# Rotating images by 90 degrees: all loads ahead of the stores, on one DMA queue, through twelve reused buffers

## The chip, the cores and the metric

The kernel runs on one core of one Trainium2 chip. The metric is the device time of one execution in microseconds (us); the time before is the median of 5 runs. A profile of one execution comes beside it. Engines in the profile: DVE is VectorE, ACT is ScalarE, SP is SyncE, POOL is GpSimd. Here only DVE computes; SP and ACT do nothing but issue DMAs, and the DMA engines, 16 of them, carry the data between HBM and SBUF.

## What is computed

A batch of 32 images with 3 channels of 256 x 256 float32 is rotated clockwise, each of the 96 planes by itself:

```python
batch, c, h, w = 32, 3, 256, 256
x = np.random.randn(batch, c, h, w).astype(np.float32)
out = np.rot90(x, k=-1, axes=(-2, -1)).astype(np.float32)
```

So out[i, j] = x[255 - j, i] in each plane: no arithmetic, 25.17 MB in and 25.17 MB out.

## The kernel before

The 96 planes are cut into 12 slabs of 8 planes, 2 MB each; the loop `for n in range(n_slabs)` takes one after the other. A slab passes through three steps.

Load (L47): two DMAs of 1 MB from SP's queue. Each fills every second partition of the input tile, 64 of them, with 16 consecutive rows of a plane, which is one run of 16 KB (`RI` = 16 rows of 256 floats).

Turn (L53): 8 transposes on VectorE, one for each c of `RO` = 8. A transpose works on blocks of 32 x 32 inside a group of 32 partitions; 512 elements of each partition go into one. The access patterns of source and destination do the rest: the destination is written backwards, which makes a rotation out of the transposition. The output tile holds, for each half `i` of the slab, 8 consecutive output rows in each of 128 partitions.

Store (L56): two DMAs of 1 MB from ACT's queue, each with 128 runs of 8 KB.

Tiles come from two pools, `in_pool` and `out_pool`, of 6 buffers each (16 KB in a partition, 192 KB together). The first 6 slabs can be loaded without waiting for a buffer; slab 6 goes into the buffer of slab 0, and so has to wait until slab 0 has been turned. The turn of slab 6 likewise waits until slab 0 has been stored. The order on each queue is the program's: SP holds 24 loads, ACT 24 stores, and each queue's instructions are issued in order, one standing until what it waits for has come. The framework that sets the waits hands out 8 completion semaphores for DMAs in turn; a DMA that gets a semaphore that is still in use waits for the DMA that used it before. With both queues drawing from the 8, SP has 6 loads on their way before it waits for the first.

Of the kernel before, what the change touches and what calls it, by code (L numbers as in the profile page):

```python
# [1 line left out]

# [4 lines left out]


@with_exitstack  # L10
def kernel(
    ctx: ExitStack,
    tc: tile.TileContext,
    x: bass.AP,
    out: bass.AP,
):

    nc = tc.nc
    fp32 = mybir.dt.float32

    B, C, H, W = x.shape
    P = nc.NUM_PARTITIONS
    RI, RO = 16, 8  # L30
    K, G = H // RI, H // RO
    I = 2
    Q = P // (K * I)
    n_slabs = B * C // (Q * I)

    ld_v = x.rearrange("b c h w -> (b c h) w").rearrange(
        "(n i m r) w -> n i m (r w)", i=I, m=Q * K, r=RI)
    st_v = out.rearrange("b c h w -> (b c h) w").rearrange(
        "(n i p c) w -> n i p (c w)", i=I, p=P, c=RO)

    in_pool = ctx.enter_context(tc.tile_pool(name="in_pool", bufs=6))
    out_pool = ctx.enter_context(tc.tile_pool(name="out_pool", bufs=6))

    for n in range(n_slabs):
        t_in = in_pool.tile([P, RI * W], fp32, tag="t_in")
        for i in range(I):
            nc.sync.dma_start(out=t_in[i::I], in_=ld_v[n, i])  # L47

        t_out = out_pool.tile([P, I, RO * W], fp32, tag="t_out")
        src = t_in.rearrange("p (r g c) -> p c r g", r=RI, c=RO)  # L50
        dst = t_out.rearrange("p i (c k r) -> p c r k i", c=RO, r=RI)[:, :, ::-1, ::-1, :]
        for c in range(RO):
            nc.vector.transpose(out=dst[:, c], in_=src[:, c])  # L53

        for i in range(I):
            nc.scalar.dma_start(out=st_v[n, i], in_=t_out[:, i])  # L56


# [1 line left out]
_INS = ['x']  # L60
_OUTS = [((32, 3, 256, 256), 'float32')]


# [23 lines left out]
```

## Time and profile before

| | |
|---|---|
| median of 5 runs | 124.46 us (124.43 to 124.56) |
| the profiled execution | 124.43 us |
| its span in the profile | 122.6 us |
| VectorE busy | 96.3 us in 96 transposes, 1091 ns mean |
| DMA | 50.34 MB, mean 410 GB/s over the span |
| loads: issue to landing, median | 15.0 us |
| stores: issue to landing, median | 12.5 us |
| SP's issue of a load | 472 ns median, 617 longest |
| ACT's issue of a store | 338 ns median, 1225 longest |
| first load issued | 0.73 us |
| first transpose starts | 8.45 us |
| first store issued | 16.65 us |

The span runs from the first to the last instruction of the profiled execution. Consecutive transposes overlap, so that 96 of them take 96.3 us and not 96 times their mean. In the profile's row of 40 slices a slice is 3.066 us; a digit is the busy share in tenths, 9 standing for 90% and more. In a list of waits the columns are: who waited for what, total us, how many times, the longest.

### The profile page before, as it was taken

To read this page: it belongs to the slowest core of one execution; us is meant where nothing else is said; L and a number is where in the kernel's file an instruction comes from. 1 tells how busy PE (TensorE), PEld (TensorE's weight loads), DVE (VectorE), ACT (ScalarE), POOL (GpSimd) and SP (SyncE) were. 2 spreads that over 40 slices of the span, in tenths; PEclk is the share of its full clock that TensorE was granted. 3 is DMA by queue.
4 is the path that set the end of the run, shared out by engine and by line. 5 is a ranking of instruction groups with operands and counts; after the bars stand their busy time and mean duration, and the time that the engine had idled before them with its cause. 6 is when DMAs were issued, how large, how long until landed. Compare 5 with 4: busy or idle time off the path is not lost.

```text
span 122.6 us, 225 instructions
## 1 busy us (share of the span) xinstructions
DVE 96.3 (79%) x96; POOL 0.2 (0%) x4
## 2 busy tenths in 40 slices
DVE  0029999999999999999999999999999999100000
POOL 0000000000000000000000000000000000000000
DMA  3999999999999999999999999999999999999993
GB/s 85 422 428 428 428 433 339 428 433 409 428 449 428 409 444 430 425 436 411 449 428 428 425 430 444 428 412 425 428 428 428 428 428 428 428 428 428 428 428 160
DMA packets 5377, 50.34 MB, mean 410 GB/s; under 512 B 768, under 2 KB 768, under 8 KB 768
## 3 DMA queue, kind: packets, MB, share of 16 engines
q1 hardware_dynamic: 1920, 25.17, 48.9%
q10 hardware_dynamic: 3456, 25.17, 48.6%
q14 instruction: 1, 0.01, 0.0%
HBM read 25.17 MB, written 25.17 MB: 410 GB/s over the span
## 4 chain that ended last, share of the span: by engine, by line
DMA 58%; DVE 24%; DVEq 1%; issue 1%; SPq 0%; ACTq 0%
DMA out_dram<-t_out 53%; DVE t_out L53 24%; DMA t_in<-in_x_dram 6%; DVEq L82 1%; SPq L47 0%; ACTq L56 0%; DVEq L53 0%
## 5 line engine op out<-in xcount | busy, mean ns | idle before, releaser
L53 DVE STREAM_TRANSPOSE t_out<-t_in 128x512 f32<-128x512 f32 x96 | 96.3, 1091 | 8.5 <-DMA t_in<-in_x_dram 8.5
L71 POOL MEMSET const-bfloat16-1.0<- 128x1 bf16 x1 | 0.1, 102 | 0.0
L71 POOL MEMSET const-uint8-127<- 128x1 uint8 x1 | 0.1, 102 | 0.0
L71 POOL MEMSET const-float32-0.0<- 128x1 f32 x1 | 0.1, 99 | 0.2 <-issue 0.2
L71 POOL MEMSET const-float32-1.0<- 128x1 f32 x1 | 0.1, 99 | 0.0
## 6 DMA issues: line engine op xcount, KB each, us to landing
t_in<-in_x_dram SPq DMA_DIRECT2D x24, 1024.0 KB, 15.0
out_dram<-t_out ACTq DMA_DIRECT2D x24, 1024.0 KB, 12.5
```

The source lines that it names most:

```text
L53: nc.vector.transpose(out=dst[:, c], in_=src[:, c])
L71: nc = _bacc.Bacc("TRN2", target_bir_lowering=False, num_devices=1)
L82: with _tile.TileContext(nc) as tc:
```

## The change

The two pools become 12 single buffers of 16 KB in a partition, `units`, the same 192 KB. Slab n is loaded into unit n, for n = 0 to 10, before anything else is issued; no load waits for a buffer. Slab n is turned out of unit n into unit n - 1, which the turn of slab n - 1 has just read; slab 0 is turned into unit 11. Each slab is stored from the unit into which it was turned. Slab 11 is loaded into unit 11, after slab 0 has been stored from it; this load is issued behind the stores of slabs 0 and 1.

All DMAs are now issued by SP: 22 loads, 5 stores (slab 0 has three, since its first half is cut into a piece of 1 KB and one of 7 KB in each partition), 2 loads, 20 stores. ACT's queue is empty. With 8 semaphores for one queue, each DMA from the ninth on waits for the one 8 places before it, apart from what it waits for otherwise.

Slab 0 has a layout of its own: each half is loaded into one half of the unit, with 8 rows (a run of 8 KB) in each of 128 partitions, and is turned by two transposes of 1024 elements a partition, of which the first waits only for its half. So slab 0 has 4 transposes instead of 8; the other slabs have 8 as before. On VectorE the first transpose of each later slab also waits for the last of the slab before.

```diff
-    ld_v = x.rearrange("b c h w -> (b c h) w").rearrange(
-        "(n i m r) w -> n i m (r w)", i=I, m=Q * K, r=RI)
-    st_v = out.rearrange("b c h w -> (b c h) w").rearrange(
-        "(n i p c) w -> n i p (c w)", i=I, p=P, c=RO)
+    N_UNITS = 12
+    rows_in = x.rearrange("b c h w -> (b c h) w")
+    rows_out = out.rearrange("b c h w -> (b c h) w")
+    ld8_v = rows_in.rearrange("(n i p r) w -> n i p (r w)", i=I, p=P, r=RO)
+    ld16_v = rows_in.rearrange("(n i m r) w -> n i m (r w)", i=I, m=Q * K, r=RI)
+    st_v = rows_out.rearrange("(n i p c) w -> n i p (c w)", i=I, p=P, c=RO)
 
-    in_pool = ctx.enter_context(tc.tile_pool(name="in_pool", bufs=6))
-    out_pool = ctx.enter_context(tc.tile_pool(name="out_pool", bufs=6))
+    pools = [ctx.enter_context(tc.tile_pool(name=f"unit{u}", bufs=1)) for u in range(N_UNITS)]
+    units = [p.tile([P, RI * W], fp32, name=f"u{u}") for u, p in enumerate(pools)]
 
-    for n in range(n_slabs):
-        t_in = in_pool.tile([P, RI * W], fp32, tag="t_in")
+    def load(n, t):
         for i in range(I):
-            nc.sync.dma_start(out=t_in[i::I], in_=ld_v[n, i])
+            if n == 0:
+                nc.sync.dma_start(out=t.rearrange("p (i f) -> p i f", i=I)[:, i], in_=ld8_v[n, i])
+            else:
+                nc.sync.dma_start(out=t[i::I], in_=ld16_v[n, i])
 
-        t_out = out_pool.tile([P, I, RO * W], fp32, tag="t_out")
+    def turn(n, t_in, t_out):
+        if n == 0:
+            for i in range(I):
+                fs = slice(i * RO * W, (i + 1) * RO * W)
+                src = t_in[:, fs].rearrange("p (r g c) -> p c r g", r=RO, c=RO)
+                dst = t_out[:, fs].rearrange("p (c g r) -> p c r g", c=RO, r=RO)
+                dst = dst[:, :, ::-1, ::-1]
+                for h in range(2):
+                    cs = slice(h * RO // 2, (h + 1) * RO // 2)
+                    nc.vector.transpose(out=dst[:, cs], in_=src[:, cs])
+            return
         src = t_in.rearrange("p (r g c) -> p c r g", r=RI, c=RO)
-        dst = t_out.rearrange("p i (c k r) -> p c r k i", c=RO, r=RI)[:, :, ::-1, ::-1, :]
+        dst = t_out.rearrange("p (i c k r) -> p c r k i", i=I, c=RO, r=RI)[:, :, ::-1, ::-1, :]
         for c in range(RO):
             nc.vector.transpose(out=dst[:, c], in_=src[:, c])
 
+    def store(n, t):
         for i in range(I):
-            nc.scalar.dma_start(out=st_v[n, i], in_=t_out[:, i])
+            src = t.rearrange("p (i f) -> p i f", i=I)[:, i]
+            cuts = [0, W, RO * W] if n == i == 0 else [0, RO * W]
+            for a, b in zip(cuts, cuts[1:]):
+                nc.sync.dma_start(out=st_v[n, i][:, a:b], in_=src[:, a:b])
+
+    last = N_UNITS - 1
+    for n in range(n_slabs - 1):
+        load(n, units[n])
+    for n in range(n_slabs):
+        turn(n, units[n], units[(n - 1) % N_UNITS])
+        store(n, units[(n - 1) % N_UNITS])
+        if n == 1:
+            load(n_slabs - 1, units[last])
```

## The prediction

> **What bounds the kernel now.** I read the page first: busy time by engine, then the slices, then the queues.
>
> ```profile
> DVE 96.3 (79%) x96; POOL 0.2 (0%) x4
> ...
> DVE  0029999999999999999999999999999999100000
> ...
> DMA  3999999999999999999999999999999999999993
> GB/s 85 422 428 428 428 433 339 428 433 409 428 449 428 409 444 430 425 436 411 449 428 428 425 430 444 428 412 425 428 428 428 428 428 428 428 428 428 428 428 160
> ...
> q1 hardware_dynamic: 1920, 25.17, 48.9%
> q10 hardware_dynamic: 3456, 25.17, 48.6%
> ```
>
> The DMA row is 9 in every slice but the first and the last: the 16 DMA engines are what the kernel runs at. VectorE (DVE) is idle for the first 8 us and the last 18. Loads (q1) and stores (q10) move 25.17 MB each, and together their packets fill 97.5% of the engines' span. What a change can win is therefore not inside the 38 full slices, except where the rate falls: slice 6 (from 18.4 us) has 339 where its neighbours have 428 to 433. The rates on either side of 428 further on (409 beside 449) cancel.
>
> The chain of waits should not mislead here:
>
> ```profile
> DMA out_dram<-t_out 53%; DVE t_out L53 24%; DMA t_in<-in_x_dram 6%; DVEq L82 1%; SPq L47 0%; ACTq L56 0%; DVEq L53 0%
> ```
>
> It gives VectorE 24%, but the slices show DMA full beside those transposes; nothing becomes shorter by shortening them.
>
> Next I cut the span at the places where the traffic changes its kind, and asked for the busy time of each stretch (columns: stretch, length, DVE, POOL, clock, DMA share, GB/s).
>
> ```profile
> 0.00:2.00 2.00, 0.00 (x0) 0.20 (x4) 1.00 0.00 0
> 2.00:3.20 1.20, 0.00 (x0) 0.00 (x0) 1.00 0.87 218
> 3.20:18.20 15.00, 9.75 (x10) 0.00 (x0) 1.00 1.02 433
> 18.20:24.20 6.00, 6.00 (x7) 0.00 (x0) 1.00 0.96 370
> 24.20:54.20 30.00, 30.00 (x31) 0.00 (x0) 1.00 1.01 431
> 54.20:84.20 30.00, 30.00 (x31) 0.00 (x0) 1.00 1.01 428
> 84.20:120.20 36.00, 20.58 (x21) 0.00 (x0) 1.00 1.01 427
> 120.20:122.60 2.40, 0.00 (x0) 0.00 (x0) 1.00 0.23 96
> ```
>
> From 3.2 to 18.2 us only loads run, from 24.2 to 84.2 loads and stores mixed on two queues, from 84.2 on almost only stores. The three rates, 433, 431 and 428, 427, differ by no more than packets at the edges of a stretch explain, so I take one rate for all, 429 GB/s. With it the span is accounted for: 2.0 us before the first byte; 0.59 lost in the 1.2 us at 218; 50.33 MB / 429 = 117.3; the dip around 18 to 24 us; and at the end 2.4 us that move only 0.23 MB (0.54 us' worth), so 1.86. The dip I price on the slices, whose edges fall better: slices 1 to 7 average 415.1 against 428.5, over 7 x 3.066 us that is 0.67. Sum 2.0 + 0.59 + 117.3 + 0.67 + 1.86 = 122.4, and 0.2 that I cannot place, to the span of 122.6. That profiled execution took 124.43 us, so 1.83 lie around the span; the median of the runs is 124.46, no different.
>
> Last, who waits:
>
> ```profile
> SPq L47 <- DMA t_in<-in_x_dram: 57.7, 18, 6.3
> SPq L82 <- DMA out_dram<-t_out: 50.4, 4, 43.2
> ```
> ```profile
> DVE t_out L53 <- DMA t_in<-in_x_dram: 8.5, 1, 8.5
> ```
>
> SyncE's queue (SP) waits 57.7 us for earlier loads while DMA is full: it is simply ahead. These waits are free, and VectorE waits only for the first slab.
>
> **The change part by part.**
>
> *The traffic.* Bytes are the same. Loads: 22 of 24 keep their 16 KB runs; slab 0's two load with 8 KB runs. Stores: 24 become 25, 128 small (1 KB) runs are added. q10's 3456 packets of 8 KB and completions took 48.6% of the span, q1's 1920 of 16 KB and completions 48.9%, for the same bytes: run length from 8 KB up changes nothing by more than 0.3 points (0.4 us over all the data), and a twelfth of the loads is concerned, so 0.03 us. The 128 extra runs are 8 per DMA engine, 1 completion more each: at the mean length of a q10 packet (0.486 x 16 x 122.6 us / 3456 = 276 ns) that would be at most 9 x 0.28 = 2.5 us if short ones cost as much as long ones; since both queues' time goes with bytes, not packets (1920 against 3456), I take 0.03 and keep 0.5 as upper end.
>
> *The order on one queue.* The stores leave ACT's queue for SP's. The dip falls where the first stores (issued at 16.65 us) join the running loads on a second queue. In the changed kernel no two queues run together, so I take its 0.67 away; the bounds are 0.67 and nothing (if it is the first store as such that costs it, it moves to 56 us).
>
> In its place come three turns of direction in one queue: loads to stores, stores to the last load, load to stores. The trace has no such turn on one queue. The nearest row is 84.2, where mixed traffic becomes pure stores: 428 before, 427 after, and the slices there (425, 428) show no dip, so one turn costs under 0.05 us. The far one is the dip, 0.67 each, 2.0 for three. The first is nearer in kind for two of the turns; for the turn back to loads neither is. I take 0.2 for all three, with 0 and 2.0 as ends.
>
> *Where the stream could run dry.* Data start at an effective 2.6 us (2.0 + 0.59). 22 loads (23.07 MB) end at 56.4, store 0 (2.1 MB, 4.9 us) at 61.3, store 1 at 66.2, the last load at 71.1, and store n from 2 on starts at 71.1 + 4.9 x (n - 2): store 11 at 115.2, its end at 120.1.
>
> The last load is a new wait: it fills unit 11, which store 0 reads, so SP stands until store 0 has landed, and behind it in SP's order are stores 2 to 11. What covers it is store 1, issued ahead and worth 4.9 us. Needed: landing, at most about 0.9 us after the last byte (two loads, 4.9 us of data from 2.6, end at 7.5; VectorE starts at 8.45), 0.5 for SP's issue (median 472 ns), and 1.3 from the first issue (0.73) to the first bytes (2.0): 2.7. Price nothing, reserve 2.2. Without cover it would cost those 2.7. [...]
>
> Beyond that SP carries 49 issues: 24 loads at 0.47 us, 25 stores at ACT's 338 ns (median) to 1225 (longest): 20 to 42 us in all, of 120. Each DMA from the ninth on waits for the one eight before it; eight megabyte transfers are 19.6 us of queued work, more than the 15.0 median to landing with which the queue is full today. Price nothing.
>
> *VectorE.* It starts earlier, since slab 0's halves are turned one by one: first half in at 2.6 + 2.45 + 0.9 = 6.0. Its four transposes of 1024 elements are not in the trace; by elements they are twice 1.003 us (96.3 / 96), together 8.0. Slab 0 ends near 14. The other 11 take 8.03 each, and each now waits for the one before to finish, 0.15 more (a transpose lasts 1091 ns and the next starts after 1003): the last ends near 104, against 115.2 when its store's turn comes. 11 us of reserve cover every sensible price of the new shape: even at twice the time it is 8 more. Nothing.
>
> *Loads alone.* The stretch with loads alone grows from 15 us to 54. The row says 433 for 15 us, and I keep 429. [...]
>
> *Start and end.* The first load has 128 runs instead of 64, so its engines may fill sooner or later: -0.1, bounds -0.3 and +0.1. The tail's 1.86 includes engines that finish one after another; without the dip they should stay closer: -0.1, bounds -0.4 and +0.3.
>
> **Sum.** 122.6 - 0.67 + 0.03 + 0.03 + 0.2 - 0.1 - 0.1 = 122.0; plus 1.83: 123.8 us. Its own range, without the far ends, is 123.2 to 124.2.
>
> **The rivals.**
>
> *Nothing changes.* The dip belongs to the first stores, not to the second queue, and comes at 56 us instead. For it: it lies exactly at the first stores. Against it: the stores were issued two microseconds earlier, and the loads were what moved in it. 122.0 + 0.67 = 122.7, 124.5 us. Chance 0.18.
>
> *Each turn costs a dip.* Place: 56.4, 66.2 and 71.1 us, where the queue changes direction. Price 0.67 each, 2.0 in all instead of the 0.2: 123.8, so 125.6 us. It decides from 0.35 each on: 1.05 in all takes up the 0.8 that the other terms win and 0.25 more. For it: the only dip of the trace is at a change of kind. Against it: the change at 84 us shows none. Chance 0.13.
>
> *A stall at the last load, or slower loads.* If store 0 lands over 2.2 us later than assumed, each microsecond beyond costs one; loads at 415 (the mean of slices 1 to 7) instead of 429 would cost 23.07 / 415 - 53.8 = 1.8: 125.6 us. The 15 us at 433 speak against it. Chance 0.07.
>
> **How the numbers follow.** The forecast holds 0.62. Two tenths of a per cent are 0.25 us, what a measurement of this kernel can tell from no change. Forecast counts as faster, the first rival as the same, the other two as slower; a little of the forecast's upper range reaches the same: 0.60, 0.20, 0.20. The range goes from 123.1 (gains at their bounds: 122.6 - 0.67 - 0.3 - 0.4 = 121.2, plus 1.83 = 123.1) to 125.1, which takes in the first rival and part of the second.
>
> **What would show it.** Slices near 428 GB/s all through, without one near 339; at 56, 66 and 71 us no slice under 415; the first two loads landing by 8.4 us; VectorE done near 104; no waiting of SP at the last load that leaves a DMA slice under 9. A dip at 56 us alone makes the first rival right, three dips the second; a hole at 66 us means that the cover was too short.

## The result, and the profile after

The changed kernel takes 124.91 us (median of 24 runs, 124.21 to 125.68) against 124.51 for the kernel before (45 runs, 124.40 to 124.75). The ratio is 1.0031, 95% interval 1.0022 to 1.0039: slower by 0.3%, where 123.8 and a gain had been forecast. The profiled execution took 125.02 us with a span of 123.0.

Most of this 0.40 us lies outside the span. The median span of the changed kernel is 122.8 us, that of the kernel before 122.7; the time around the span, 1.73 to 1.83 us in every execution of the kernel before that was timed beside an experiment, is 1.76 to 2.23 here, median 2.03. What makes these 0.2 us more is not shown.

The page of the profile after, the same rows as shown of before:

```profile
DVE 97.5 (79%) x92; POOL 0.2 (0%) x4
...
DMA  3999999999999999998999999999999999999993
GB/s 104 426 450 426 426 426 426 437 437 426 426 432 432 426 432 426 426 384 344 426 426 432 405 410 426 429 429 426 426 426 426 426 432 426 426 426 426 429 429 149
...
q1 hardware_dynamic: 5648, 50.33, 97.6%
```

DMA is full throughout, as before, but for one slice of 8. The dip of slice 6 is gone from its place, and stands in slices 17 and 18 (52 to 58 us: 384, 344), where the queue passes from loads to stores. A second, flatter one is in slices 22 and 23 (405, 410), where slab 11's load stands among the stores. Cut at these places (stretch, length, DVE, POOL, clock, DMA share, GB/s):

```profile
0.00:2.00 2.00, 0.00 (x0) 0.20 (x4) 1.00 0.10 33
2.00:3.20 1.20, 0.00 (x0) 0.00 (x0) 1.00 0.78 239
3.20:18.20 15.00, 12.54 (x9) 0.00 (x0) 1.00 1.02 434
18.20:53.50 35.30, 35.16 (x36) 0.00 (x0) 1.00 1.01 429
53.50:58.00 4.50, 4.46 (x5) 0.00 (x0) 1.00 0.97 340
58.00:66.50 8.50, 8.46 (x9) 0.00 (x0) 1.00 1.03 434
66.50:72.50 6.00, 5.97 (x7) 0.00 (x0) 1.00 0.99 400
72.50:120.20 47.70, 30.92 (x31) 0.00 (x0) 1.00 1.01 427
```

Against 429 GB/s the first dip loses 4.5 x (1 - 340/429) = 0.93 us and the second 6.0 x (1 - 400/429) = 0.41. The first bytes come at 1.74 us now; the kernel before moved nothing until 2.04. Loads alone run at 434 and 429, stores alone at 427.

What this mean over 16 engines hides is in the trace's packets. Each DMA ends on each engine with a 4-byte packet; their times say when the first and the last of the 16 engines were through with it (worked out from the trace of after):

```
DMA on SP's queue                first engine  last engine  apart, us
21st load                        53.53         54.10        0.57
22nd load                        56.58         57.10        0.52
store 0, second piece (7 KB)     59.07         59.91        0.84
store 1, second half             66.43         67.26        0.84
slab 11's load, first half       68.89         70.33        1.44
slab 11's load, second half      71.35         72.76        1.41
store 2, first half              73.81         75.22        1.41
last store                      120.41        121.82        1.41
```

Undisturbed, a megabyte takes 2.45 us on every engine. The dip is there already in the 22nd load, the last one ahead of the stores: 3.0 us for the first engine and for the last. For the first half of slab 11's load the first engine needed 2.46 (66.43 to 68.89) and the last 3.07. Followed packet by packet, the engine that is through at 68.89 has four packets of 16 KB at 611 ns each, the one at 70.33 has one of 1279 ns among its four: one engine loses nothing, another 0.6. The store behind the load takes 2.45 again, so the loss lies in the change from stores to the load and not in the one after it. From then on the distance stays at 1.41: no engine makes its lateness good, and the kernel ends with the last. In the kernel before the last store's 16 packets lie between 120.56 and 121.50, 0.94 apart.

### The profile page after: what moved, and what is told of

It is laid out like the page before. It is cut to its first block, busy times and chain, and to the rows that moved or that the text cites. A ratio compares the mean times of both kernels' runs of the same rounds, so it can differ in the third digit from the quotient of the medians.

```text
span 123.0 us, 212 instructions
## 1 busy us (share of the span) xinstructions
DVE 97.5 (79%) x92; POOL 0.2 (0%) x4
## 4 chain that ended last, share of the span: by engine, by line
DVE 71%; issue 8%; DMA 4%; DVEq 1%
DVE u L74 65%; DVE u L69 6%; DMA u<-in_x_dram 4%; DVEq L116 1%
## 5 line engine op out<-in xcount | busy, mean ns | idle before, releaser
L74 DVE STREAM_TRANSPOSE u<-u 128x512 f32<-128x512 f32 x88 | 89.7, 1106 | 0.4
L69 DVE STREAM_TRANSPOSE u<-u 128x1024 f32<-128x1024 f32 x4 | 7.8, 2051 | 5.6 <-DMA u<-in_x_dram 5.6
```

Of the source, the lines that this page charges most:

```text
L69: nc.vector.transpose(out=dst[:, cs], in_=src[:, cs])
```

## The experiments

Each kernel was timed beside the kernel before (medians of 124.50 to 124.53 there); the interval is that of the ratio to it. Diffs are against the changed kernel where nothing else is said. The dip is the fall of the rate at the first stores; the turn back is the queue's change from stores to the load of slab 11 (not the transposing of a slab, which is also called a turn).

### Taking the change apart

**The queue.** Stores on ACT's queue, all else as changed:

```diff
-                nc.sync.dma_start(out=st_v[n, i][:, a:b], in_=src[:, a:b])
+                nc.scalar.dma_start(out=st_v[n, i][:, a:b], in_=src[:, a:b])
```

> The changed kernel with its stores on ACT's queue again, each as soon as it is turned; units, slab 0 and the loads stay. Theory (first stores cost one dip, wherever they meet running loads; the turn back to loads inside one queue costs the late half of the DMA engines 0.5 to 0.6 more): a dip of 0.6 to 0.7 between 14 and 21 us, no slow packets at the last load, time 124.2 to 124.5. Rival (units or the loads far ahead are what costs): 124.8 to 125.1, as the changed kernel.

124.22 us, 0.9974 (0.9965 to 0.9984). Its stretches, in the same columns:

```profile
15.00:18.00 3.00, 3.00 (x4) 0.00 (x0) 1.00 0.95 335
...
66.00:72.00 6.00, 6.00 (x7) 0.00 (x0) 1.00 1.01 426
```

The dip at the first stores is there (3 x (1 - 335/429) = 0.66 us); where the changed kernel had 400 there is 426. The single queue costs 124.91 - 124.22 = 0.7 us, of which the median spans (122.8 and 122.4) show 0.4; units and early loads are not what costs.

**Slab 0's layout, alone in the kernel before:**

```diff
         for i in range(I):
-            nc.sync.dma_start(out=t_in[i::I], in_=ld_v[n, i])
+            if n == 0:
+                nc.sync.dma_start(out=t_in.rearrange("p (i f) -> p i f", i=I)[:, i], in_=ld8_v[n, i])
+            else:
+                nc.sync.dma_start(out=t_in[i::I], in_=ld_v[n, i])
...
+        if n == 0:
...
+            continue
```

> The kernel before with slab 0 in the changed kernel's layout (two loads of 128 runs of 8 KB, four transposes, each half stored by itself). In the changed kernel the first bytes came at 1.74 us instead of 2.04, but half of the engines began at 2.6 as before. If the mean of the engines counts: 124.5 - 0.3 = 124.2. If the late half counts: 124.4 to 124.5.

124.21 us, 0.9975 (0.9964 to 0.9985): the earlier start is worth 0.3 us, by the mean of the engines, and the rival that only the late half counts falls.

**Units and early loads alone:** stores on ACT's queue, and slab 0 like the other slabs (its special branches and the division of its first store made void).

> Twelve units and the loads far ahead, stores on ACT's queue, slab 0 as every other slab: what is left of the change when the queue and slab 0's layout are undone. If units and early loads are worth nothing: 124.4 to 124.6, the time before. If they win what slab 0's layout seemed to win: 124.2.

124.52 us, 1.0001 (0.9992 to 1.0009). Twelve units and loads far ahead are worth nothing. With two_queues at 124.22 this is the 0.3 of slab 0's layout a second time.

**Slab 0 undone on the one queue:** the same branches made void, stores on SP.

> The changed kernel with slab 0 loaded, turned and stored as every other slab (no 8 KB runs at the start, no 1 KB piece). If the early start is a gain: 125.2. If it only sets half of the engines ahead of the other half and the last engine sets the end: 124.8 to 125.0, with engine ends closer together.

125.07 us, 1.0037 (1.0024 to 1.0051). The interval overlaps the changed kernel's, so this run tells neither theory.

### The load of slab 11

**On ACT's queue:**

```diff
-                nc.sync.dma_start(out=t[i::I], in_=ld16_v[n, i])
+                eng = nc.scalar if n == n_slabs - 1 else nc.sync
+                eng.dma_start(out=t[i::I], in_=ld16_v[n, i])
```

> The changed kernel with the load of slab 11 issued from ACT's queue instead of SP's; it still waits for store 0 to land, but now runs beside the stores on a second queue, so SP's queue never turns from stores back to loads. Theory (this turn back inside one queue costs the last engine 0.6): 124.2 to 124.4, the spread of the 16 engines' completions stays near 0.85 us after 60 us instead of growing to 1.4. Rival (any load that begins among stores costs it, whatever the queue): 124.8 to 125.0.

124.21 us (12 runs), 0.9976 (0.9964 to 0.9987): two DMAs moved to the idle queue give back all of the 0.7 (0.5 in the median spans, 122.8 and 122.3). What was expected of the spread can't be read: the profiled execution was the slowest of the twelve (124.73), and its engines ended 1.42 us apart. The time is shown, the picture of it not.

**Left out** (slab 11 is turned from another unit, so the output lacks it and 2.1 MB are not loaded):

> The changed kernel without the load of slab 11 (its turn reads another unit): 2.1 MB less to carry, which at the loads' pace is 4.87 us, and the two changes of direction at 66 to 71 us gone. If these two changes cost the 0.3 that slow packets suggest: 124.9 - 4.87 - 0.3 = 119.7. If they cost nothing: 120.0. If the wait for store 0 cost more than that: below 119.5.

119.31 us (119.17 to 119.37). 124.91 - 119.31 = 5.60, of which 4.87 are the bytes: 0.73 for the two changes of direction, as with the move to ACT, and more than the mean over the engines suggests. The median span is 117.35, which leaves 122.8 - 117.35 - 4.87 = 0.6 inside the span, near what the last engine lost.

**Issued behind store 4 instead of store 1** (`if n == 4`):

> The changed kernel with the load of slab 11 issued behind store 4 instead of store 1: store 0 has landed long before, so SP waits for nothing there and the queue holds its usual eight transfers; the turn from stores to a load and back remains, near 81 us. If the turn itself costs the 0.7 that moving this load to ACT's queue saved: 124.8 to 125.2, slow packets at the load near 81 to 86 us. If SP's wait for store 0 and the short queue behind it cost it: 124.2 to 124.4.

124.67 us (124.14 to 125.54), 1.0016 (1.0000 to 1.0033).

```profile
58.00:78.00 20.00, 19.93 (x21) 0.00 (x0) 1.00 1.01 428
78.00:88.00 10.00, 9.93 (x10) 0.00 (x0) 1.00 1.01 410
88.00:120.20 32.20, 15.40 (x16) 0.00 (x0) 1.00 1.01 428
```

The loss moved along with the load, to 78 to 88 us (10 x (1 - 410/429) = 0.44), though nothing waits for store 0 there: SP's longest wait for a store at that load is 2.1 us, where it is 8.3 in the changed kernel. The interval lies above last_load_act's, so the turn costs without any wait. Whether the wait for store 0 adds the remaining 0.24 stays open: the intervals of this and of the changed kernel overlap.

### The first stores

**Slab 0's store and slab 11's load placed elsewhere:**

```diff
-    for n in range(n_slabs - 1):
+    for n in range(n_slabs // 2):
         load(n, units[n])
+    turn(0, units[0], units[last])
+    store(0, units[last])
+    for n in range(n_slabs // 2, n_slabs):
+        load(n, units[n])
...
```

> The changed kernel with slab 0's store issued behind 6 slabs of loads instead of 11, and the load of slab 11 behind the other loads, ahead of store 1. Changes of direction: loads to store near 35 us, back to loads near 40, loads to stores near 61. Theory A (once, at the first store): 0.7 near 35 us, little at 61; 0.3 for the turn back to loads at most; 124.6 to 125.0. Theory B (each load-to-store change): 0.7 at 35 and 0.7 at 61 us; 125.2 to 125.6.

125.62 us, 1.0083 (1.0061 to 1.0104).

```profile
27.00:30.00 3.00, 2.96 (x4) 0.00 (x0) 1.00 0.98 399
30.00:33.00 3.00, 3.00 (x4) 0.00 (x0) 1.00 0.96 287
33.00:39.00 6.00, 5.97 (x6) 0.00 (x0) 1.00 1.04 438
39.00:42.00 3.00, 3.00 (x4) 0.00 (x0) 1.00 0.97 350
...
66.00:71.00 5.00, 4.97 (x6) 0.00 (x0) 1.00 1.01 428
```

1.2 us are lost at the first stores, 0.55 at the return to loads, and nothing shows at the second change from loads to stores (428). By the packets that change lies at 66.6 to 68.5 us, not near 61 as expected, and the store behind it takes 2.45 us on the first engine (69.04) and on the last (70.97). The places are those of theory A; the prices are above what it gave.

**Store n and load n + 6 in turn, after six slabs of loads:**

> The changed kernel with 6 slabs of loads first and then store n, load n+6 in turn on the one queue: 6 changes from load to store more or less like the one at 56 us, and 6 back. Theory A: one dip of 0.7 at the first store, the others at 0.1 to 0.3 for each pair: 125 to 126.5. Theory B: 0.7 to 1.0 for each pair, 6 or 7 of them: 129 to 131. If turns in one queue cost nothing at all: 124.5.

125.92 us, 1.0113 (1.0097 to 1.0128).

```profile
27.00:33.00 6.00, 5.97 (x7) 0.00 (x0) 1.00 0.97 349
33.00:39.00 6.00, 5.97 (x6) 0.00 (x0) 1.00 1.04 437
39.00:42.00 3.00, 3.00 (x4) 0.00 (x0) 1.00 1.03 393
42.00:90.00 48.00, 47.80 (x48) 0.00 (x0) 1.00 1.01 425
```

The first change costs 6 x (1 - 349/429) = 1.1, the first return 0.25, and all later ones together, over 48 us at 425, about 0.45. A price for each change, theory B, would be several times that.

**Small stores first.** Three kernels let 0.07 to 0.13 MB be stored ahead: small_first issues the 1 KB piece on ACT's queue, piece_same_queue on SP's behind slab 5's loads, warm_act (the before_8k kernel) stores zeros on ACT's queue ahead of everything, which slab 0's store overwrites.

```diff
+    warm = warm_pool.tile([P, 128], fp32, name="warm")
+    nc.vector.memset(warm, 0.0)
+    nc.scalar.dma_start(out=st_v[0, 0][:, 0:128], in_=warm)
```

> The changed kernel with one edit: the piece of 1 KB a partition of slab 0's first store is issued from ACT's queue as soon as it is turned (near 10 us), so a store of 0.13 MB runs long before the others. Theory A (the dip is a price of the first store to HBM, paid once): the dip at 54 to 57 us is gone or under 0.2, time 124.2 to 124.4. Theory B (the dip is a price of each change from a long run of loads to stores in one queue): a dip of about 0.7 at 54 to 57 us stays, time 124.8 to 125.1.

> The changed kernel with the 1 KB piece of slab 0's first store (0.13 MB) issued on SP's queue behind the loads of slab 5, the rest of the stores where they were. If a queue pays once for its first store of any size: a loss of 0.1 to 0.2 near 32 us, the dip at 54 to 57 us under 0.2, time 124.3 to 124.6. If it takes a full-sized store: the dip of 0.7 at 54 to 57 us stays, time 124.9 to 125.3.

> The kernel before with slab 0 in the new layout, and a small store (128 x 512 B, 0.07 MB, zeros that slab 0's store overwrites) on ACT's queue ahead of everything. If the first store of a queue pays the dip whatever its size and time: the dip at 12 to 15 us is gone and 124.2 becomes 123.6 to 123.8. If the dip comes with full-sized stores among running loads: 124.2 to 124.4, the dip stays.

125.14, 125.40 and 124.48 us. The dip stays in all three (slices of 350, 339 and 361 GB/s at the first full stores), so a small store doesn't pay it, on its own queue or on the other. None of the three is faster than the kernel that it was made from (124.91, 124.91 and 124.21).

**All of slab 0's store on ACT's queue, the rest on SP's:**

> The changed kernel with all of slab 0's store (2.1 MB) on ACT's queue as soon as it is turned, the rest as it was; the order on SP's queue is loads 0 to 10, store 1, load 11, stores 2 to 11. If the dip is paid once by the first full-sized store, on whatever queue: 0.6 to 0.7 at 12 to 20 us, under 0.15 at 58 us. If each queue pays at its own first store: two dips, 125.4 to 125.7. The turn back to loads (store 1 to load 11) stays in both.

126.46 us, 1.0156 (1.0126 to 1.0185), above both expectations.

```profile
12.00:18.00 6.00, 5.97 (x6) 0.00 (x0) 1.00 0.99 377
...
30.00:36.00 6.00, 6.00 (x7) 0.00 (x0) 1.00 0.97 388
...
57.00:63.00 6.00, 5.96 (x7) 0.00 (x0) 1.00 0.99 350
63.00:69.00 6.00, 6.00 (x7) 0.00 (x0) 1.00 0.98 414
69.00:75.00 6.00, 5.96 (x7) 0.00 (x0) 1.00 1.00 386
```

Two dips: 0.73 at ACT's first stores, 1.1 at SP's, and 0.8 over the last two stretches, at slab 11's load. Another 0.57 goes at 30 to 36 us, just after the last packet of ACT's store (30.45), where SP's loads run alone again; neither expectation had it, and it stays unexplained. With early_store and alternate, where one queue shows its dip only once, the two dips suggest that each queue pays at its own first full-sized stores.

### The length of the loads' runs

**All slabs in slab 0's layout,** loads of 8 KB runs, on one queue and on two:

> The changed kernel with every slab in slab 0's layout (loads of 128 runs of 8 KB, four transposes of 1024 elements), one queue as before. If the losses at the changes of direction come from the loads' 16 KB runs on 64 partitions: dip and turn shrink by half or more, 124.0 to 124.4. If not: 124.8 to 125.3, with a dip of 0.6 to 0.8 near 56 us and slow packets at 66 to 71 us.

> All slabs in slab 0's layout, stores on ACT's queue. If the dip at the first stores comes from the loads' 16 KB runs: 123.6 to 123.9. If not, as the same kernel with 16 KB loads: 124.1 to 124.4.

125.20 us, 1.0065 (1.0048 to 1.0083), and 124.72 us, 1.0020 (1.0011 to 1.0029). On one queue:

```profile
18.20:53.50 35.30, 35.30 (x20) 0.00 (x0) 1.00 1.01 422
53.50:58.00 4.50, 4.50 (x3) 0.00 (x0) 1.00 1.01 412
58.00:66.50 8.50, 8.50 (x5) 0.00 (x0) 1.00 1.02 429
66.50:72.50 6.00, 6.00 (x5) 0.00 (x0) 1.00 1.01 426
```

Dip and turn are all but gone (412, 426, where the changed kernel has 340 and 400), yet the loads run at 422 instead of 429 for 50 us, and the kernel is no faster. In the profiled execution the last packet ends 0.13 us earlier than in the changed kernel's (121.70 and 121.83), but 1.63 us of the span lie behind it instead of 1.15, which is not explained either. On two queues the dip stays (a slice of 350).

**Only the loads next to stores in that layout:** slabs 10 and 11, or slab 10 alone.

> The changed kernel with slabs 10 and 11 also in slab 0's layout: the loads that stand next to stores in the queue now have 128 runs of 8 KB, all others keep 64 runs of 16 KB. If only 16 KB loads next to stores in one queue lose time: no dip at 54 to 57 us, no slow packets at 66 to 71, time 123.4 to 123.8, under both kernels. If what rows8 showed came from 8 KB loads all along: dip and turn come back, 124.8 to 125.0.

> The changed kernel with slab 10, the last load ahead of the first stores, in slab 0's layout, slab 11 not. By the theory the dip at 54 to 57 us goes and the turn back at slab 11 stays: 124.1 to 124.4, between the changed kernel and rows8_at_turns. If the two losses are one: as one of the two others.

124.95 us, 1.0038 (1.0024 to 1.0052), and 124.84 us, 1.0022 (1.0010 to 1.0035): the changed kernel's time, with both losses in place. Of rows8_at_turns:

```profile
53.50:58.00 4.50, 4.47 (x5) 0.00 (x0) 1.00 0.99 350
...
66.50:72.50 6.00, 5.97 (x7) 0.00 (x0) 1.00 1.02 418
```

The mean at the turn back is higher than in the changed kernel (418 and 400), but the last engine again needs 3.01 us for the first half of slab 11's load, and the engines end 1.39 apart. So the runs of the loads beside the stores don't make the losses. Why a kernel with slightly slower loads throughout has none stays open.

## Why the prediction was wrong, step by step

**The step that failed** is "The order on one queue", in both its terms: the dip, taken away, stayed, and the turns, taken at 0.2, cost 0.7.

*"I take its 0.67 away".* The dip was put down to two queues running together. It goes with a queue's first full-sized stores and moved with them to 54 us, where it cost 0.93 by the slices: the term is 0, not -0.67. The first rival, "nothing changes", had this mechanism; its ground, that the dip lies exactly at the first stores, was the better reading.

*"I take 0.2 for all three" turns.* The turn from stores to slab 11's load and back cost 0.7 by the times (last_load_act against the changed kernel; 0.73 by no_last_load), 0.4 to 0.6 of it inside the span. The second rival, "Each turn costs a dip", had two of its three places right, 56 and 66 us; at the third, from the load to the next store, nothing was lost. The row taken as the nearest, at 84 us, was a queue of loads running dry beside a queue of stores, which is no turn within a queue. For the turn back the prediction had said that neither row was near; then the dip's 0.67, its other bound, should have carried the sum. The price also lies elsewhere than the prediction looked: 0.6 on the last engine, nothing on the first.

**Start, -0.1:** right in sign, mis-sized: 0.3 measured, twice (before_8k; two_queues against two_queues_plain), at the bound given. **Tail, -0.1:** wrong: the engines end 1.41 us apart instead of 0.94, by the same turn; without it they end 0.86 apart (no_last_load). **Around the span, 1.83:** the changed kernel has 2.03, and the forecast had no reason to expect it.

The sum with the measured terms: 124.51 - 0.3 (start) + 0 (dip) + 0.7 (turn, with what it changes around the span) = 124.9, the 124.91 measured. The 0.7 is itself a difference to 124.91; what the sum shows is that nothing else is left over, as last_load_act and two_queues do, which have the early start and no turn back and take 124.51 - 0.3.

**The wait for store 0** was covered as worked out. SP issued the last load at 62.83 us, while store 1 kept the queue busy until 66.4 on the first engine:

```profile
62.83 1.66 SPq L58 DMA_DIRECT2D u<-in_x_dram  x2
64.58 40.57 SPq L81 DMA_DIRECT2D out_dram<-u  x20
```

3.6 us were left; less the 0.5 for the issue and the 1.3 to the first bytes, both as the prediction took them, that is a reserve of 1.8 where 2.2 had been worked out. Store 0's last packet ended at 62.36, so SP went on within 0.5 us of it, not the 0.9 taken. **Loads alone** kept their rate, 434 and 429 GB/s over 50 us, where 429 had been taken. **The small runs** cost little, as taken: a 1 KB packet lasts 46 ns in the trace and a 7 KB one 272, against 309 for the 8 KB packet that they replace; with 8 of them on each engine and a completion packet of 9 ns that is 0.08 us, where 0.03 had been taken. **VectorE** ended near 104 us; only one store's issue waited for it, 3.4 us, with the DMA engines full:

```profile
L74 DVE STREAM_TRANSPOSE u<-u 128x512 f32<-128x512 f32 x88 | 89.7, 1106 | 0.4
L69 DVE STREAM_TRANSPOSE u<-u 128x1024 f32<-128x1024 f32 x4 | 7.8, 2051 | 5.6 <-DMA u<-in_x_dram 5.6
```

The transposes of 1024 elements take 7.8 us together (8.0 estimated). Each later slab took 0.15 more than 8.03, as forecast, though the two durations given for it, 1091 and 1003 ns, make only 0.09.

The steady rate is the same on one queue and on two: 427 GB/s for the stores of the changed kernel, 426 for the loads and stores of two_queues. The total time differs: the same bytes with the stores on a second queue are 0.7 us faster. Between the first slice and the last the DMA row has no digit under 8 in either, so this is not issue time; what it comes with is the change of direction within the queue.

Beyond that, three versions beat the kernel before by the same 0.3 us of slab 0's layout (before_8k 124.21, last_load_act 124.21, two_queues 124.22); the simplest is the kernel before with the new first slab. All loads ahead of all stores, without the turn back, was not tried; it would need a thirteenth unit of 16 KB in a partition.

## What to carry to other kernels

A change of direction inside one DMA queue is not free because the same change between two queues was (427 GB/s behind 428 at 84 us of the kernel before, yet 0.7 us for the turn to slab 11's load and back): price it by its own row, and where there is none, let the far bound into the sum. When DMA sets the end, look at the last of the 16 engines as well as at the mean; what one engine lost in the middle, 0.6 us here, was still lost at the end (1.41 us between the first engine and the last from slab 11's load on). Compare spans beside times: what lies around the span can change too (1.73 to 1.83 us before, a median of 2.03 after), and no row of the profile shows it. A dip that coincides with two things (a second queue, the first stores) should be left in the sum until one of them is ruled out.

## What the runs showed of the hardware that had not been expected

- At the turn back to a load, the first engine needed 2.46 us for a megabyte and the last 3.07; the distance they then had, 1.41 us, stayed constant over the 48 us that followed.
- A queue's first full-sized stores cost 0.7 to 1.2 us of DMA time, on ACT's queue and on SP's, and later changes from loads to stores on the same queue little (428 GB/s from 66 to 71 us in early_store, 0.45 us for all of them in alternate, with the returns); small stores ahead did not spare it (slices of 350, 339 and 361 GB/s). One kernel, with all loads in 8 KB runs on one queue, did not show it (412 GB/s from 53.5 to 58 us). The cause is not found.
- Runs scatter more on the one queue (124.21 to 125.68) than with stores on the other (two_queues: 124.11 to 124.28). Without slab 11's load four runs lie within 0.20 us (no_last_load), with that load alone on the other queue twelve spread over 0.75 (last_load_act). What makes the scatter was not shown.
- The time around the span, steady at 1.73 to 1.83 us in the kernel before, has a median of 2.03 in the changed kernel and 1.79 in two_queues. The cause is not found.
